# Unit length of queries and keys as columns in a gated DeltaNet mixer

## The chip, the cores and the metric

The kernel runs on one core of one Trainium2 chip. The metric is the device time of one execution in microseconds (us), shown as the median of several runs. A profiled execution is one further run of the same program, with its instructions recorded. "Span" is the time from its first to its last instruction; the execution's own time is a little longer.

## What is computed

A decoder trunk of two layers on 272 tokens (16 learned ones and 256 given) of width 1024. Each layer is a mixer and then a mixture of experts (MoE) whose weights fill most of the memory traffic. The change is in the second layer's mixer, a gated DeltaNet with 8 heads of queries and keys, 16 of values, width 128:

```python
q, k, v = jnp.split(jax.nn.silu(causal_depthwise_conv(qkv, conv_w)), ...)
q = jnp.repeat(l2_normalize(q.reshape(B, T, 8, 128)), 2, axis=2)   # x * rsqrt(sum(x*x) + 1e-6)
k = jnp.repeat(l2_normalize(k.reshape(B, T, 8, 128)), 2, axis=2)
g, beta = -exp(a_log) * softplus(a + dt_bias), sigmoid(b)
# per chunk of 64 tokens, gc = cumsum(g), decay[i,j] = exp(gc_i - gc_j):
m   = tril((k * beta) @ k.T * decay, -1)
sol = triangular_solve(m + eye, [v * beta, k * beta * exp(gc)])     # -> u, w
v_new = u - w @ S
o     = (q * 128**-0.5 * exp(g)) @ S + (q * 128**-0.5) @ k.T * decay @ v_new
S     = S * exp(g_last) + (k * exp(g_last - g)).T @ v_new
```

The output o then goes through an RMS norm per head, a gate and the output projection.

## The kernel before

All engines work from one program that is issued in a written order; each engine runs its own part of it in that order. The engines: PE (matrix products into PSUM), DVE (VectorE), ACT (ScalarE), POOL (GpSimd), SP (issues the transfers).

`mixer1` runs 48 projections of 128 columns, numbered m: keys' heads (m = 0 to 7), queries' heads (8 to 15), values (16 to 31), gates z (32 to 47). Each is 24 matmuls (`proj3`, line 361), since the operands are split into a high and a low part: ACT or DVE writes the high part of a weight tile (lines 72 and 74, `HI1`), mostly POOL the low part (line 347, `LO1`), two projections ahead (`ahead`). Weight tile 20 is written into the memory that the squares of the queries (tile `s`) held before. After projection m, `conv` copies the result to SBUF (ACT, line 838), takes the four taps of the short convolution (ACT line 840, DVE three times line 842), and the silu of the result before it (ACT, line 856) writes the head to `qk` and gives the PSUM bank free. There are 8 PSUM banks for everything.

Between the projections, pieces of other work are issued. They are Python generators, and the table `PLAN` says after which m each takes its next step: `clear`, `places`, `residual`, `uk` = `unit(8)` (the keys' length), `ga` = `heads` (gates, strengths beta in `bt`, decays), `dec` = `decay` (POOL line 1002, PE line 1007, ACT's Exp line 1008, DVE line 1013), and `uq` = `unit(0)` (the queries' length), in this order within one m. The products of keys with keys (`keys`) come at m = 14, 15 and 17, those with queries (`queries`) at 23 to 26 (both line 1029), the transposed keys (`key_rows`) at 15 to 19, the transposed values (`value_rows`, line 1217, scaled by beta in line 1221) at 21, 25 and 31 and after. From m = 15 the triangular systems are solved on DVE in the background (`systems`, `system0`, paced by `tick`), then joined on PE (`merges`, lines 1150 to 1186, with DVE's line 1166 between). After projection 33 the recurrence over five chunks follows (`read`, `solve`, `write`), in between the rest of the z projections and the first transfers of MoE weights into memory that has become free, then the output projection, then the MoE.

`unit(i0)` normalises eight heads in nine steps. In four steps ACT squares two heads each (line 882). In the fifth, PE sums each head's squares over the partitions into one row of a bank (line 888), ACT takes Ln and Exp(-0.5 x) of the 128 x 272 result (lines 892 and 893; each needs another activation table), and DVE splits the factor into a high and a low part (lines 74 and 347, tile `sq`). In the last four, for each head two matmuls with a column of `sel8` spread its factor over all partitions (line 899), and DVE multiplies the head by it (line 902).

`heads` picks the gates of the heads out as columns by small products with the identity (line 918) and ends with `nbe`, minus decay times beta (line 955). In the recurrence `nbe` scales what is read from the state (line 1306), `eg` the queries' part (line 1308), and line 1351 adds that to the part inside the chunk.

Of the kernel before, what the change touches and what calls it, by code (L numbers as in the profile page):

```python
# [8 lines left out]
F32 = mybir.dt.float32  # L9
# [4 lines left out]
OP = mybir.AluOpType  # L14
# [30 lines left out]
HX = 24  # L45
EXTRA = (3, 1, 1, 1, 1, 3)
NTS = 650
PLAN = ((0, 0, 1, 1, 3), (1, 4), (6, 10), (5, 6, 7, 8, 9, 11, 12, 13, 13), (0, 0, 2, 3, 7, 8), (6, 8, 9, 10, 11), (11, 13, 14, 16, 18, 20, 21, 22, 22))
HI1 = 'aaaaaaaavavvvaavaaaaaaaaaaaaaaavaavavaaaaavavaaa'
LO1 = 'ppppppppppppppppppppppppppppppppppvvppppppppppvp'  # L50
ZN = 21
# [2 lines left out]
class Trunk:  # L54
# [24 lines left out]
    def constants(self):  # L79
# [30 lines left out]
        nc.gpsimd.memset(self.col, 0.0)  # L110
        nc.gpsimd.memset(self.col[:, 1:2], 1.0)
        self.ones = self.col[:, 1:2].to_broadcast([128, 128])
        self.sel8 = c.tile([128, 8], F32, name="sel8")
        nc.vector.tensor_copy(self.sel8.bitcast(F32R).rearrange("p (a g) -> p g a", a=2),
                              self.ident.rearrange("p (g a) -> p g a", g=4)[:, :, 0:2])
        self.neghalf = c.tile([128, 2], F32, name="neghalf")
        nc.gpsimd.memset(self.neghalf, -0.5)
        self.lnst = c.tile([128, 3, 4, 6], F32, name="lnst")
# [622 lines left out]
    def mixer1(self):  # L741
# [10 lines left out]
        def tl(shape, name, bufs=1, pl=None):  # L752
            return (pl or qp).tile(shape, F32, tag=name, name=name, bufs=bufs)
# [12 lines left out]
        Abd, qk = cut(ab_, 0, (5, 8, 128)), cut(qk_, 0, (16, T))  # L766
        ktok = [cut(ab_, 5120, (4, 128)), cut(ab_, 5632, (4, 128))] + [cut(tk, 512 * i, (4, 128)) for i in range(3)]
        g, gs, nbe = cut(tk, 1536, (5, 8)), tk[:, 1576:1736], tk[:, 1736:1776]
        bvs = {}

        def bv(c, h, n=1):
# [99 lines left out]

        def unit(i0):

            ts = slice(0 if i0 else 16, T)
            if i0:
                s = [tl([128, 640], f"vt{i // 2}", 2, ep) for i in range(4)]
                s = [s[i // 2][:, T * (i % 2):T * (i % 2) + T] for i in range(8)]
            else:
                s = self.half(0, "s").rearrange("p (h t) -> p h t", h=8)
                s = [s[:, i, :] for i in range(8)]  # L880
            for i in range(8):
                nc.scalar.activation(s[i][:, ts], qk[:, i0 + i, ts], AF.Square)
                if i % 2:
                    yield
            p = self.ps()
            for i in range(8):
                a, r = i // 4, 32 * (i % 4)
                nc.tensor.matmul(p[r:r + 32, ts], self.col[:, 1 - a:33 - a], s[i][:, ts], start=(a == 0), stop=(a == 1),
                                 skip_group_check=True)
            f = tl([128, T], "cv", 1, ep)[:, ts]  # L890
            fh, fl = (tl([128, T], "sq", 2, ep)[:, ts] for _ in range(2))
            nc.scalar.activation(f, p[:, ts], AF.Ln, bias=eps6)
            nc.scalar.activation(f, f, AF.Exp, scale=-0.5)
            self.split(fh, fl, f, "v", "v")
            yield
            for i in range(8):
                p = self.ps()
                for a in (fh, fl):
                    nc.tensor.matmul(p[:, ts], self.sel8[:, i:i + 1].to_broadcast([128, 128]).bitcast(F32R),
                                     a.bitcast(F32R), start=(a is fh), stop=(a is fl))  # L900
                o = qk[:, i0 + i, ts]
                V.scalar_tensor_tensor(o, o, 1.0 if i0 else 128.0 ** -0.5, p[:, ts], op0=OP.mult, op1=OP.mult)
                if i % 2:
                    yield

        def heads():

# [44 lines left out]
            V.tensor_sub(gs[:, 40:80], pg[:, 40:80], gs[:, 0:40])  # L952
            yield
            nc.scalar.activation(gs, gs, AF.Exp)
            V.scalar_tensor_tensor(nbe, gs[:, 0:40], -1.0, bt.rearrange("p c h -> p (c h)"), op0=OP.mult, op1=OP.mult)
            yield

        eg, egl, eS = gs[:, 0:40], gs[:, 40:80], gs[:, 80:160]

        def residual():  # L960

# [100 lines left out]
        def system0():  # L1062
# [3 lines left out]
            nc.gpsimd.memset(M0, 0.0)  # L1066
            unit_matrix(X0, 16)
            yield 1200
            V.tensor_copy(b0[:, 0:8], bt[:, 0, :])
            bs0 = tl([128, 32], "bs", 1, pp)  # L1070
            V.transpose(out=bs0, in_=b0)
            for hf in range(2):
# [30 lines left out]

        def systems():

            V.transpose(out=bs, in_=bt[:, 1:5, :].rearrange("p c h -> p (c h)"))
            V.transpose(out=Ms, in_=KT[:, :, 0:32].rearrange("p s i -> p i s"))
            yield 2000

# [24 lines left out]
            for hf in range(2):  # L1134
                r0, r1 = slice(64 * hf, 64 * hf + 32), slice(64 * hf + 32, 64 * hf + 64)
                V.transpose(out=M21[r1], in_=KT[r0, :, 32:64])
                nc.gpsimd.tensor_tensor(M21[r1], M21[r1], bt[r1, 1:5, :].rearrange("p c h -> p (c h)")[:, :, None]
                                        .to_broadcast([32, 32, 32]), op=OP.mult)
                yield 1200

# [69 lines left out]
        def value_rows(b):  # L1210
            for c0 in (0, 2, 4):
# [6 lines left out]
                for c in range(c0, c0 + cn):  # L1218
                    for j in range(2):
                        o = 256 * (c - c0) + 128 * j  # L1220
                        nc.scalar.activation(bv(c, 2 * b + j)[:, 0, :], p[:, o:o + 128], AF.Copy,
                                             scale=bt[:, c, 2 * b + j:2 * b + j + 1])

        nz = [0]

# [103 lines left out]
        def write(c, b):  # L1329
# [18 lines left out]
                nc.tensor.matmul(pv[:, 256 + 128 * s:384 + 128 * s], Abd[:, c, 2 * b + s, :], vn[:, s, :],  # L1348
                                 start=True, stop=True)
            o = bv(c, 2 * b, 2)  # L1350
            V.tensor_tensor(o, pv3[:, 2:4], yd, op=OP.add)
            t3 = st[c, b] = tl([128, 3, 2], "ost", 3, rp)
            for s in range(2):
                junk = tl([128, 128], "junk", 2, rp)
# [871 lines left out]
```

## Time and profile before

| | us |
|---|---|
| median of 3 runs | 1351.94 |
| lowest and highest run | 1349.91, 1352.54 |
| profiled execution, own time | 1349.69 |
| its span | 1347.9 |
| busy in the span: PE, PEld | 1192.5, 694.3 |
| busy in the span: DVE, ACT, POOL | 452.6, 341.6, 204.7 |
| mean granted PE clock | 0.935 of 2.4 GHz |

PE is the matmuls, PEld the loads of their weights, which overlap them. A line number is one of the listing; a helper's line (72, 74, 347, 361) stands for all its callers. A matmul of full float32 operands is recorded as two instructions. In a timeline a row is a group of equal instructions: start, length, engine, line, operation, tiles, shape, count, and in brackets how long the engine had stood idle before and what ended that. Groups of matmuls overlap their neighbours, so the time that one takes is read from start to start.

### The profile page before, as it was taken

The numbers are of one execution on the slowest core, as the hardware profiler recorded it, in microseconds if no ns is written. First come the engines' busy times: TensorE is split into PE (matmuls) and PEld (weight loads), VectorE is DVE, ScalarE is ACT, GpSimd is POOL, SyncE is SP. The second block draws the span as 40 slices with busy tenths as digits, with TensorE's granted clock in tenths as the row PEclk, the third lists the DMA queues.
The fourth block names the chain that finished last, engine by engine and source line by source line (L and its number), as shares of the span: only waits on it lengthen the run. The fifth ranks groups of instructions, "written<-read, shape, count | busy, mean of one in ns | idle before, by whom it ended". The sixth has DMA issues, their size and how long they took to land. (4 is left out here: it accounts for less than half of the span.)

```text
span 1347.9 us, 19704 instructions
## 1 busy us (share of the span) xinstructions
PE 1192.5 (88%) x8074; PEld 694.3 (52%) x8074; DVE 452.6 (34%) x1035; ACT 341.6 (25%) x739; POOL 204.7 (15%) x183
## 2 busy tenths in 40 slices
PE   9999998898899799899999999899787868968786
PEld 9877544242435244378888878784231323414132
DVE  4876321010110201148987376653010010101013
ACT  4763110000100000057575645432010010101001
POOL 5621000000000000048754453000000000000000
PEclk9999998979697987999998999999999998998889
DMA  8599799999999999934333344979999999999996
GB/s 265 151 344 361 293 417 423 423 427 424 421 425 426 424 424 426 383 112 154 103 117 97 126 157 164 389 290 407 421 427 427 427 425 424 426 426 427 427 424 245
DMA packets 129844, 454.92 MB, mean 338 GB/s; under 512 B 19667, under 2 KB 62390, under 8 KB 94918
## 3 DMA queue, kind: packets, MB, share of 16 engines
q1 hardware_dynamic: 129590, 452.95, 84.4%
q8 instruction: 67, 1.10, 0.3%
q10 hardware_dynamic: 144, 0.52, 0.1%
q14 instruction: 43, 0.35, 0.1%
HBM read 452.39 MB, written 1.05 MB: 336 GB/s over the span
## 5 line engine op out<-in xcount | busy, mean ns | idle before, releaser
L1907 PE MATMUL ps<-Sg,h 128*128 128x128 f32 (+1 forms) x640 | 170.4, 409 | 11.8 <-ACTq L2179 11.5
L1907 PEld LDWEIGHTS ps<-Sg,h 128*128 128x128 f32 (+1 forms) x640 | 143.4, 291 | 56.9 <-issue 30.1
L1931 PE MATMUL ps<-w,xg 128*32 128x512 f32 x456 | 137.1, 636 | 10.3 <-DMA w<-in_moe_w_up_dram 10.0
L2037 DVE TENSOR_TENSOR acc<-acc,ps 128x512 f32<-128x512 f32 x48 | 33.0, 688 | 234.4 <-PE ps L2028 234.4
L347 POOL TENSOR_TENSOR w<-w 128x1024 fp32r<-128x1024 f32 x14 | 33.3, 2380 | 477.0 <-ACT w L72 467.7
L295 DVE TENSOR_SCALAR xg<-ps,pg 128x128 f32<-128x128 f32 x66 | 24.2, 406 | 219.2 <-PE ps L1907 218.0
L1952 DVE TENSOR_TENSOR y<-y,ps 128x512 f32<-128x512 f32 x16 | 11.0, 688 | 225.9 <-PE ps L1931 225.9
L253 POOL TENSOR_SCALAR lnmv<-lnmv 128x1 f32<-128x1 f32 (+2 forms) x9 | 2.6, 294 | 523.8 <-DVE lnmv L320 523.2
L1931 PE MATMUL ps<-wr,xg 128*32 128x512 f32 x320 | 80.2, 655 | 1.4 <-DMA wr<-in_moe_w_up_dram 1.4
L2028 PE MATMUL ps<-y,ct 128*128 128x512 f32 (+1 forms) x170 | 77.1, 584 | 2.1 <-ACT y L72 2.1
L1931 PE MATMUL ps<-we,xg 128*32 128x512 f32 x304 | 71.3, 620 | 7.1 <-DMA we<-in_moe_w_up_dram 7.1
L361 PE MATMUL ps<-xh,ws 128*128 128x272 f32 (+2 forms) x496 | 73.1, 293 | 2.7 <-ACT ws L72 2.6
L293 ACT ACTIVATE xg<-ps,pg 128x128 f32<-128x128 f32 x62 | 25.1, 453 | 190.0 <-PE ps L1907 190.0
L1931 PE MATMUL ps<-wb,xg 128*32 128x512 f32 x264 | 71.2, 677 | 0.5 <-DMA wb<-in_moe_w_up_dram 0.5
L347 POOL TENSOR_TENSOR ws<-w,ws 128x1024 fp32r<-128x1024 f32 x26 | 61.9, 2387 | 56.1 <-ACT ws L72 43.5
L361 PEld LDWEIGHTS ps<-xh,ws 128*128 128x128 f32 (+1 forms) x496 | 65.4, 189 | 4.5 <-ACT ws L72 2.8
L1931 PE MATMUL ps<-tb,xg 128*32 128x512 f32 x152 | 60.2, 627 | 5.6 <-DMA tb<-in_moe_w_up_dram 5.6
L1931 PEld LDWEIGHTS ps<-w,xg 128*32 128x32 f32 x456 | 31.2, 116 | 64.5 <-issue 45.5
L72 ACT ACTIVATE hT<-ps 128x512 f32<-128x512 f32 x16 | 9.6, 597 | 199.9 <-PE ps L1956 199.9
L1989 PE MATMUL ps<-w,hT 128*32 128x512 f32 x144 | 52.3, 652 | 8.7 <-DMA w<-in_moe_w_down_dram 8.0
L72 ACT ACTIVATE y<-ps 128x512 f32<-128x512 f32 (+1 forms) x34 | 19.4, 572 | 153.8 <-PE ps L1989 125.0
L842 DVE SCALAR_TENSOR_TENSOR ps<-xp,cw,ps 128x272 f32<-128x272 f32 (+1 forms) x96 | 47.6, 498 | 21.7 <-ACT ps L840 20.0
(518 smaller groups left out, 2266.5 us busy)
## 6 DMA issues: line engine op xcount, KB each, us to landing
w<-in_moe_w_up_dram SPq DMA_DIRECT2D x34, 1024.0 KB, 19.6
w<-in_odd_w_in_dram SPq DMA_DIRECT2D x24, 1024.0 KB, 5.2
w<-in_moe_w_gate_dram SPq DMA_DIRECT2D x23, 1024.0 KB, 19.6
wr<-in_moe_w_gate_dram SPq DMA_DIRECT2D x22, 1024.0 KB, 17.9
we<-in_moe_w_down_dram SPq DMA_DIRECT2D x22, 1024.0 KB, 17.9
we<-in_moe_w_gate_dram SPq DMA_DIRECT2D x20, 1024.0 KB, 10.6
wr<-in_moe_w_down_dram SPq DMA_DIRECT2D x20, 1024.0 KB, 19.6
wr<-in_moe_w_up_dram SPq DMA_DIRECT2D x18, 1024.0 KB, 21.1
```

The costliest lines, as they stand in the source:

```text
L72: self.nc.scalar.activation(out, in_, AF.Copy)
L293: self.nc.scalar.activation(out, in_, AF.Identity, scale=g, bias=b)
L295: self.nc.vector.tensor_scalar(out, in_, g, b, op0=OP.mult, op1=OP.add)
L347: e.tensor_tensor(lo.bitcast(F32R), x, hi, op=OP.subtract)
L361: self.nc.tensor.matmul(p[0:m, t0:T], w[:, k, 0:m], x[:, k, n0:], start=(n == order[0] and k == 0), stop=(n == order[2] and k == 7))
L842: V.scalar_tensor_tensor(cv, x[:, j + t0:j + T], w(j), cv, op0=OP.mult, op1=OP.add)
L1907: nc.tensor.matmul(p[:, 128 * j:128 * j + 128], self.rows(k.H(t), k0 + j, gr), Sg[0:P, t].rearrange("p e c -> p (e c)"), start=(t == 1), s ...
L1931: nc.tensor.matmul(pp[s, :], xg[:, kk + r, s], w[:, j, r, :], start=(kk + r == 0), stop=(kk + r == 7), skip_group_check=True)
L1952: V.tensor_tensor(hid, hid, pu, op=OP.mult)
L1989: nc.tensor.matmul(pys[h][s, :], hT[:, kf + r, s], w[:, j, r, 512 * h:512 * h + 512], start=(kf + r == 0), stop=(kf + r == 3), skip_group_ ...
L2028: nc.tensor.matmul(p, ct[:, t0:t0 + P], y, start=not (end and t), stop=True, skip_group_check=bool(end and t))
L2037: V.tensor_add(a, a, parts[t])
```

## The change

Queries and keys stay as the convolution gives them. `unit` copies the sums of squares to SBUF (tile `f`), and in the next step picks them out, token by partition and head by column, with small products whose weights are 64 columns of `f`; it takes Ln and Exp of 40 (keys) or 32 (queries) columns. For the keys this gives `bt2`, beta over the squared length, in place of beta in the systems and in `nbe`, and `bt1`, beta over the length, in place of beta for the values. For the queries it gives `fq`, one over the length times 128^-0.5, which goes into `eg` and into line 1351. `sel8` goes, and `PLAN` changes for `unit`, which now has seven steps, and for no other generator.

```diff
-PLAN = ((0, 0, 1, 1, 3), (1, 4), (6, 10), (5, 6, 7, 8, 9, 11, 12, 13, 13), (0, 0, 2, 3, 7, 8), (6, 8, 9, 10, 11), (11, 13, 14, 16, 18, 20, 21, 22, 22))
+PLAN = ((0, 0, 1, 1, 3), (1, 4), (6, 10), (5, 6, 7, 8, 9, 10, 11), (0, 0, 2, 3, 7, 8), (6, 8, 9, 10, 11), (11, 13, 14, 16, 17, 18, 19))
-        self.sel8 = c.tile([128, 8], F32, name="sel8")
-        nc.vector.tensor_copy(self.sel8..., self.ident...)
+        bt1, bt2, fq = (tk[:, o:o + 40] for o in (1776, 1816, 1856))
...
-            f = tl([128, T], "cv", 1, ep)[:, ts]
-            fh, fl = (tl([128, T], "sq", 2, ep)[:, ts] for _ in range(2))
-            nc.scalar.activation(f, p[:, ts], AF.Ln, bias=eps6)
-            nc.scalar.activation(f, f, AF.Exp, scale=-0.5)
-            self.split(fh, fl, f, "v", "v")
+            f = tl([128, T], "cv", 1, ep)
+            nc.scalar.activation(f[:, ts], p[:, ts], AF.Copy)
             yield
-            for i in range(8):
-                p = self.ps()
-                for a in (fh, fl):
-                    nc.tensor.matmul(p[:, ts], self.sel8[:, i:i + 1].to_broadcast([128, 128]).bitcast(F32R),
-                                     a.bitcast(F32R), start=(a is fh), stop=(a is fl))
-                o = qk[:, i0 + i, ts]
-                V.scalar_tensor_tensor(o, o, 1.0 if i0 else 128.0 ** -0.5, p[:, ts], op0=OP.mult, op1=OP.mult)
-                if i % 2:
-                    yield
+            p, c0 = self.ps(), 0 if i0 else 1
+            for c in range(c0, 5):
+                for hf in range(2):
+                    pick = self.ident.rearrange("p (z q j) -> p q j z", z=2, q=2)[:, hf, 0:2, :, None]
+                    nc.tensor.matmul(p[64 * hf:64 * hf + 64, 8 * c:8 * c + 8], f[:, CST[c]:CST[c] + 64],
+                                     pick.to_broadcast([128, 2, 2, 2]), start=True, stop=True, skip_group_check=True)
+            p = p[:, 8 * c0:40]
+            nc.scalar.activation(p, p, AF.Ln, bias=eps6)
+            if i0:
+                nc.scalar.activation(bt2, p, AF.Exp, scale=-1.0)
+                nc.scalar.activation(bt1, p, AF.Exp, scale=-0.5)
+                yield
+                b40 = bt.rearrange("p c h -> p (c h)")
+                V.tensor_tensor(bt2, bt2, b40, op=OP.mult)
+                V.tensor_tensor(bt1, bt1, b40, op=OP.mult)
+                V.scalar_tensor_tensor(nbe, eg, -1.0, bt2, op0=OP.mult, op1=OP.mult)
+            else:
+                nc.scalar.activation(fq[:, 8:40], p, AF.Exp, scale=-0.5)
+                yield
+                V.tensor_scalar(fq[:, 8:40], fq[:, 8:40], 128.0 ** -0.5, None, op0=OP.mult)
+                V.tensor_tensor(eg[:, 8:40], eg[:, 8:40], fq[:, 8:40], op=OP.mult)
+            yield
...
-            V.scalar_tensor_tensor(nbe, gs[:, 0:40], -1.0, bt.rearrange("p c h -> p (c h)"), op0=OP.mult, op1=OP.mult)
...
-            V.tensor_tensor(o, pv3[:, 2:4], yd, op=OP.add)
+            V.scalar_tensor_tensor(o, pv3[:, 2:4], fq[:, j:j + 1], yd, op0=OP.mult, op1=OP.add)
```

In `system0`, `systems` (and its M21) `bt` becomes `bt2`, and in line 1221 it becomes `bt1`; shapes stay.

## Rows read from the trace of the kernel before

**Rows 1.** The page's slices: the span in 40 equal parts, each digit the busy share in tenths; DMA is the mean busy share of the 16 DMA engines.

```profile
PE   9999998898899799899999999899787868968786
...
DMA  8599799999999999934333344979999999999996
```

**Rows 2.** Busy time by stage. Columns: the stretch and its length, then busy us of PE, PEld, DVE, ACT and POOL with the number of instructions, the granted clock of PE as a share of 2.4 GHz, the DMA share and GB/s.

```profile
640.00:705.00 65.00, 60.04 (x535) 56.10 (x534) 59.06 (x129) 42.92 (x95) 41.03 (x22) 0.97 0.37 114
705.00:765.00 60.00, 58.84 (x1147) 54.61 (x1146) 36.97 (x83) 37.24 (x92) 28.02 (x19) 0.94 0.36 109
765.00:838.00 73.00, 73.00 (x554) 57.43 (x554) 46.57 (x120) 35.05 (x115) 31.85 (x33) 1.00 0.41 144
...
905.00:1310.00 405.00, 328.46 (x1862) 129.40 (x1862) 48.98 (x108) 37.79 (x75) 0.00 (x0) 0.94 1.01 421
```

**Rows 3.** Waits of SP, which issues the transfers, from 838 to 1340 us: what waited for what, us in total, times, longest. Line 1691 issues MoE weights.

```profile
SPq L1691 <- PE ps L1931: 32.6, 20, 12.1
...
SPq L1691 <- DVE xp L347: 22.1, 4, 5.8
```

**Rows 4.** Timeline of PE in the stage of the change, and its first wait in the merges. Columns: start us, us, engine, line, operation, tiles, shape, count, idle before.

```profile
635.01 3.13 PE L1007 MATMUL ps<-R,lstrict 128*128 128x512 f32 x6 [1.05 <-POOL R L1002]
...
646.50 0.60 PE L899 MATMUL ps<-sq,sel 128*128 128x272 f32 x2 [1.23 <-DVE qk L902]
646.91 2.05 PE L361 MATMUL ps<-xh,tb 128*128 128x260 f32 x8
...
651.32 1.16 PE L899 MATMUL ps<-sq,sel 128*128 128x272 f32 x8
652.99 1.22 PE L361 MATMUL ps<-xh,bv 128*128 128x260 f32 x8 [0.50 <-ACT qk L856]
...
656.06 1.55 PE L1029 MATMUL ps<-qk 128*64 128x64 f32 x32
657.54 1.22 PE L361 MATMUL ps<-xh,bv 128*128 128x260 f32 x8
...
660.62 1.15 PE L1029 MATMUL ps<-qk 128*64 128x64 f32 x32
...
674.31 1.07 PE L888 MATMUL ps<-s,col 128*32 128x256 f32 x16
...
684.97 1.27 PE L361 MATMUL ps<-xh,bv 128*128 128x272 f32 x8 [1.19 <-ACT vt L856]
...
690.07 1.31 PE L1217 MATMUL ps<-ident,vt 128*128 128x128 f32 x10 [1.37 <-ACT vt L856]
...
694.24 1.09 PE L899 MATMUL ps<-sq,sel 128*128 128x256 f32 x8
...
699.42 1.32 PE L1029 MATMUL ps<-qk 128*64 128x64 f32 x8 [0.29 <-DVE qk L902]
...
730.33 1.20 PE L1183 MATMUL ps<-TX,Ms 32*32 32x32 f32 x64 [1.16 <-DVE TX L1166]
```

**Rows 5.** Busy time in short stretches around the wait of 1.23 us; columns as in rows 2.

```profile
645.00:647.00 2.00, 0.77 (x5) 0.50 (x4) 1.93 (x6) 1.97 (x5) 2.00 (x2) 0.95 0.00 0
647.00:649.00 2.00, 2.00 (x11) 2.00 (x11) 1.94 (x4) 0.42 (x2) 2.00 (x1) 0.50 0.41 54
```

**Rows 6.** Timeline of DVE: the two splits of the factor, the keys' and the queries'.

```profile
636.00 1.12 DVE L74 CAST sq<-cv 128x272 fp32r<-128x272 f32 x1 [3.12 <-ACT cv L893]
637.15 0.44 DVE L347 TENSOR_TENSOR sq<-cv,sq 128x272 fp32r<-128x272 f32 x1
...
681.11 0.29 DVE L74 CAST sq<-cv 128x256 fp32r<-128x256 f32 x1 [0.80 <-ACT cv L893]
681.44 0.42 DVE L347 TENSOR_TENSOR sq<-cv,sq 128x256 fp32r<-128x256 f32 x1
```

**Rows 7.** Groups of DVE's instructions by line and shape, 580 to 850 us. Columns: line, engine, operation, tiles, shapes, count, then busy us and mean ns of one, then the idle time before them and what ended it.

```profile
L1306 DVE SCALAR_TENSOR_TENSOR r<-ps,tk,bv 128x128 f32<-128x128 f32 x24 | 8.3, 348 | 14.1 <-PE ps L1301 8.8 <-ACT yd L1308 5.3
...
L1351 DVE TENSOR_TENSOR bv<-ps,yd 128x256 f32<-128x256 f32 x12 | 5.0, 417 | 0.0
...
L902 DVE SCALAR_TENSOR_TENSOR qk<-qk,ps 128x272 f32<-128x272 f32 x8 | 3.0, 431 | 0.0
L902 DVE SCALAR_TENSOR_TENSOR qk<-qk,ps 128x256 f32<-128x256 f32 x8 | 2.9, 411 | 0.0
...
L244 DVE TENSOR_TENSOR ps<-ps,sp 128x40 f32<-128x40 f32 x6 | 1.2, 206 | 0.2
```

**Rows 8.** Timeline of PE where `heads` picks the gates out (line 918), with the instructions behind it.

```profile
597.75 0.76 PE L918 MATMUL ps<-ident,sq 32*64 32x16 f32 x20 [0.48 <-ACT sq L913]
598.44 1.27 PE L361 MATMUL ps<-xh,tb 128*128 128x272 f32 x8
```

**Rows 9.** Timeline of ACT: a table load and the activation behind it, and the high part of weight tile 20.

```profile
632.44 1.28 ACT L892 ACT_TABLE_LOAD   x1
633.74 0.49 ACT L892 ACTIVATE cv<-ps,eps 128x272 f32<-128x272 f32 x1
...
675.50 1.06 ACT L72 ACTIVATE ws<-w 128x1024 fp32r<-128x1024 f32 x1 [1.70 <-issue]
```

More of the change, by code (lines that the diff above doesn't have):

```diff
@@ L112, in constants @@
         self.ones = self.col[:, 1:2].to_broadcast([128, 128])
-        self.sel8 = c.tile([128, 8], F32, name="sel8")
-        nc.vector.tensor_copy(self.sel8.bitcast(F32R).rearrange("p (a g) -> p g a", a=2),
-                              self.ident.rearrange("p (g a) -> p g a", g=4)[:, :, 0:2])
         self.neghalf = c.tile([128, 2], F32, name="neghalf")
@@ L768, in mixer1 @@
         g, gs, nbe = cut(tk, 1536, (5, 8)), tk[:, 1576:1736], tk[:, 1736:1776]
+        eg, egl, eS = gs[:, 0:40], gs[:, 40:80], gs[:, 80:160]
+        bt1, bt2, fq = (tk[:, o:o + 40] for o in (1776, 1816, 1856))
         bvs = {}
@@ L954, in heads @@
             nc.scalar.activation(gs, gs, AF.Exp)
-            V.scalar_tensor_tensor(nbe, gs[:, 0:40], -1.0, bt.rearrange("p c h -> p (c h)"), op0=OP.mult, op1=OP.mult)
             yield
-        eg, egl, eS = gs[:, 0:40], gs[:, 40:80], gs[:, 80:160]
         def residual():
@@ L1068, in system0 @@
             yield 1200
-            V.tensor_copy(b0[:, 0:8], bt[:, 0, :])
+            V.tensor_copy(b0[:, 0:8], bt2[:, 0:8])
             bs0 = tl([128, 32], "bs", 1, pp)
@@ L1104, in systems @@
         def systems():
-            V.transpose(out=bs, in_=bt[:, 1:5, :].rearrange("p c h -> p (c h)"))
+            V.transpose(out=bs, in_=bt2[:, 8:40])
             V.transpose(out=Ms, in_=KT[:, :, 0:32].rearrange("p s i -> p i s"))
@@ L1136, in systems @@
                 V.transpose(out=M21[r1], in_=KT[r0, :, 32:64])
-                nc.gpsimd.tensor_tensor(M21[r1], M21[r1], bt[r1, 1:5, :].rearrange("p c h -> p (c h)")[:, :, None]
+                nc.gpsimd.tensor_tensor(M21[r1], M21[r1], bt2[r1, 8:40, None]
                                         .to_broadcast([32, 32, 32]), op=OP.mult)
@@ L1221, in value_rows @@
                         nc.scalar.activation(bv(c, 2 * b + j)[:, 0, :], p[:, o:o + 128], AF.Copy,
-                                             scale=bt[:, c, 2 * b + j:2 * b + j + 1])
+                                             scale=bt1[:, 8 * c + 2 * b + j:8 * c + 2 * b + j + 1])
         nz = [0]
```

## The prediction, on record before the change was run

> **What bounds the kernel now.** I read the slices of the profile's page first, to see which resource is full in which part; then the busy time by stage; then the timelines of PE, VectorE (DVE) and ScalarE (ACT) in the stage that the change touches; last the waits of the DMA queue, to see whether time saved there reaches the end. In the slices the reader is to see two regimes: the transfers are full in most of the span and fall to about a third in the second mixer, where PE is full instead [rows 1]. By stage, PE is busy 60.04 of the 65 us from 640 to 705, and DVE 59.06: both are near their limit, and each makes the other wait. From 705 to 838 PE is busy 131.84 of 133 us, and DVE far less; from 905 to 1310 the DMA share is 1.01 [rows 2]. So time taken off the stretch 640 to 705 is kept if PE stays the bound up to 838 and the transfers of the expert weights start earlier by as much. They do: between 838 and 1340 the DMA queue waits, besides for itself, for PE and DVE to give slots free (32.6 and 22.1 us in the largest such rows) [rows 3]. The transfers follow the compute out of the mixer; I let a microsecond saved there count as one at the end.
>
> **What goes, PE.** `unit` spreads each head's factor over the partitions by two matmuls, 32 in all (line 899). Eight keys' take 1.16 us, eight queries' 1.09 [rows 4], so 2 x 1.16 + 2 x 1.09 = 4.50 us. They also bring waits, as each pair needs a PSUM bank and DVE has to empty it: 1.23 us before the second pair of a step, and 0.29 before queries' products that need a scaled head [rows 4]. After the 1.23 us the granted clock falls from 0.95 to 0.50, that is from nearly always 2.4 to 1.2 GHz [rows 5]: the projection behind it takes 646.91 to 651.32 = 4.41 us, where one at full clock takes 657.54 to 660.62 = 3.08, a loss of 1.33 [rows 4]. Three more waits, 0.50, 1.19 and 1.37 = 3.06 us, end with the silu of a convolution (line 856), which waits for DVE or for ACT's tables [rows 4].
>
> **What goes, DVE.** Sixteen scalings (line 902): 3.0 + 2.9 = 5.9 us [rows 7]. The two splits of the factor: 1.12 + 0.44 + 0.29 + 0.42 = 2.27 us, and in front of them DVE stands still 3.12 and 0.80 us for ACT's Exp, with the convolutions of the next heads queued behind [rows 6]. Together 12.1 us of DVE's 65.
>
> **What comes, PE.** Eighteen little products pick the squares' sums out as columns. The nearest row is the same pick for the heads' gates (line 918): ten calls, 20 instructions, start 597.75, next start 598.44, so 34.5 ns each [rows 8]. Eighteen calls are 36 instructions: 1.24 us. Below it lies 0.55 us: the keys' twenty run ahead of the second decay products, where PE waits 1.05 us for POOL anyway [rows 4], so they may cost nothing, and sixteen are left. Above it lie the products of line 1029, 64 weight columns and 64 moving ones, 32 in 1.55 us: 36 x 48 = 1.74 us [rows 4]. I take 1.24, the same shape. A rule speaks for more: the Trainium skill (TensorE: Matmul & The Clock Gate, LDWEIGHTS) gives columns / 1.2 ns for a weight load, 53 ns for 64 columns, by which the picks would come to 1.9 us as an estimate. The row of the existing pick does not bear that out.
>
> **What comes, DVE.** Five small operations on 32 or 40 columns at 0.21 us [rows 7]; one of them, the negated strengths, is only moved, so four are new: 0.8 us. The copy of `sel8` at the start goes, off the path. The sum of line 1351 becomes a scalar_tensor_tensor. Before it is 417 ns; the nearest rows of the new kind are 411 ns with a constant (line 902) and, with a column but half the elements, 348 (line 1306) [rows 7]. Scaled by elements beyond the half, a column costs 420 to 460 ns. Sixteen times 0 to 0.04 us lie beside PE, which is busy all of 765 to 838 [rows 2]; only the last group's stands before the output projection: 0 to 0.1 us, I take 0.1. The strengths that the systems, the values and M21 read are of the same shape as before: nothing.
>
> **What moves.** Per unit, ACT copies 272 or 256 columns where it took Ln, and takes Ln and Exp of 40 or 32 columns one step later. The keys' Ln and Exp now stand directly before the decay's Exp, so one change to silu and back falls away, two table loads. A load is 1.28 us and the activation starts 0.02 after it [rows 9]: 2.6 us of ACT. The Trainium skill (ScalarE: Activation LUTs, What ACT_TABLE_LOAD costs) adds a drain of 1.38 us to each; no gap of that length follows the load here, and by it the queries' three loads would hold ACT longer, which speaks for rival A. The sums of the queries are taken at projection 17, not 18. They read the tile whose memory the split of weight tile 20 overwrites; ACT now waits 1.70 us for them (675.50) [rows 9], just behind the sums (674.31) [rows 4], and that wait goes. No DMA is issued by a moved step; POOL's splits stay where they are. New waits: PE's picks wait for ACT's copy of the step before; Ln waits for the picks. At the keys the copy is ready a projection early. At the queries it stands behind a silu that waits for DVE, and the next projections of PE are queued behind the picks; this may cost up to the 0.5 us that such a wait took at 652.99 [rows 4].
>
> **Sum.** PE's own work: -4.50 + 1.24 = -3.26. The waits tied to the scaled heads and the clock: -1.23 - 0.29 - 1.33 = -2.85. Of the 3.06 us on silu I take back 2.4: DVE has 12.1 - 0.8 us less in its way, but the queries' three table loads still stand in ACT's queue, and half of the 1.19 us that follows them stays. The line 1351 tail adds 0.1. Together -3.26 - 2.85 - 2.4 + 0.1 = -8.4 us. The profiled execution took 1349.69 us (span 1347.9 and 1.8 around), so it would take 1341.3; the median of the runs, 1351.94, stands 2.25 higher, and I forecast the median: 1343.5 us. Bounds: all three waits go and the keys' picks are free, -3.26 - 0.69 - 2.85 - 3.06 = -9.9; only the work goes, at the dear pick, -4.50 + 1.74 = -2.8. What is late next is PE itself in the projections.
>
> **Rivals.** *A, only PE's work goes.* The waits belong to ACT's table loads and POOL's order, and come again at other places; 0.69 to 1.74 us of picks against 4.50, and the first wait half gone: about -4, so 1348. For it: three loads stay at the queries, and POOL's 1.05 us stays [rows 4]. Against it: the largest wait and the half clock name line 902, which is gone. Chance 0.20.
> *B, the gain is given back.* PE arrives earlier at the merges and waits longer for DVE's line 1166, where it already waits 1.16 us [rows 4], or the weights' transfers do not start earlier: 0 to -2, so 1351. Against it: DVE is relieved by more than PE, and is busy only 36.97 of 60 us there [rows 2]. Chance 0.12.
> *C, slower.* The queries' picks wait for ACT's copy at projection 18, the granted clock falls as it does after the 1.23 us, and the half clock lasts through the value projections, whose small key products keep PE loosely filled. At 1.33 us per projection the gain of 8.4 is eaten after six or seven; from nine on (12.0) the kernel is slower by over 0.2%: about 1355.5. Against it: after 1.19 and 1.37 us of waiting in the same stretch no projection was slowed. Chance 0.06.
>
> **How the numbers follow.** My forecast (-6 to -12, the waits gone in most part) has 0.62, and its number is 1343.5. The low end: the bound -9.9, the 1.16 us at the merges, which a freer DVE may shorten, and 1.3 us for the spread of the median's runs (1349.91 to 1352.54), so 1339.5. The high end: rival A and the same spread, 1349.5. Outside lie most of B, all of C and a rest below. The measurement of this kernel can tell about 0.2% (2.7 us) from no change: the forecast and most of A lie beyond it, B and the end of A within. Faster 0.80, same 0.14, slower 0.06.
>
> **What would show it.** Right: PE's starts from the second decay products (635.01) to the queries' products at 699.42 [rows 4] stand 8 to 9 us closer; no half clock behind a scaled head; about 1.2 us of picks in two groups; DVE busy some 52 us where it was 59.06; everything behind earlier by the same amount, the last weights' transfers too. Wrong: PE's waits on silu as long as before (A); a longer wait for line 1166, or the main run of expert weights no earlier than before (B); granted clock 0.5 behind the queries' picks (C).

## The result: slower by 0.7%, and the profile after

| | before | after |
|---|---|---|
| median, us | 1350.39 (5 runs) | 1359.78 (5 runs) |
| lowest to highest | 1346.45 to 1352.54 | 1359.17 to 1363.22 |
| span of the profiled execution | 1347.9 | 1358.0 |

The ratio is 1.0073, with a 95% interval from 1.0057 to 1.0089. The forecast, 1343.5, lies on the wrong side, and its range ends 10 us too low.

To find where the time went I cut each span into three sections: up to the first projection of the second mixer; from there to the start of the last product of the recurrence (line 1357 of the kernel after); and the rest, which is mostly layer 1's experts. All starts are read from PE's timelines; GB/s is read from the windows 150 to 550 us (layer 0's experts) and 905 to 1300 us (layer 1's). The experiments are in the same table, since all of them are read in this way. Each set of experiments has runs of the kernel before of its own (medians 1348.95 to 1350.24 us), and each ratio is to those; two executions, one of before (1548.12 us) and one of e3 (3411.31 us), were far slower than all others and are in no ratio. "Moved by" says where the left-hand weight tiles lie in SBUF, in bytes per partition against before.

| kernel | moved by | to 1st projection | mixer | rest | GB/s, layers 0 and 1 | ratio to before, 95% |
|---|---|---|---|---|---|---|
| before | 0 | 591.0 | 251.7 | 505.2 | 422, 421 | 1 |
| after | -32 | 597.2 | 246.0 | 514.8 | 418, 416 | 1.0073 [1.0057, 1.0089] |
| e1 | 0 | 591.3 | 242.6 | 504.5 | 422, 425 | 0.9979 [0.9969, 0.9989] |
| e8 (e1 again) | 0 | 592.4 | 246.6 | 506.0 | 422, 423 | 0.9966 [0.9949, 0.9983] |
| e2 | +32 | 599.6 | 249.9 | 513.9 | 417, 416 | 1.0109 [1.0089, 1.0130] |
| e3 | -64 | 596.4 | 246.3 | 513.6 | 418, 415 | 1.0067 [1.0051, 1.0082] |
| e4 | 0 | 593.3 | 240.8 | 505.3 | 422, 425 | 0.9925 [0.9912, 0.9938] |
| e5 | -256 | 594.7 | 240.6 | 505.6 | 422, 425 | 0.9935 [0.9913, 0.9958] |
| e6 | -128 | 601.6 | 241.5 | 512.7 | 418, 417 | 1.0037 [1.0022, 1.0052] |
| e7 | -32 | 595.6 | 242.8 | 514.7 | 418, 416 | 1.0057 [1.0036, 1.0078] |
| e9 | -256, others too | 593.9 | 239.7 | 505.9 | 424, 425 | 0.9911 [0.9891, 0.9931] |
| e10 | 0 | 591.4 | 241.2 | 507.4 | 422, 425 | 0.9946 [0.9927, 0.9964] |
| e11 | 0, constants -32 | 591.3 | 242.7 | 506.3 | 422, 425 | 0.9941 [0.9922, 0.9960] |
| e12 | 0 | 592.4 | 257.7 | 505.6 | 422, 423 | 1.0070 [1.0047, 1.0094] |

After against before: +6.2, -5.7 and +9.6 us, together the +10.1 by which the spans differ. The mixer, the only place where arithmetic changed, did become shorter. The loss lies in the two sections that the forecast did not look at. Sections are of one profiled execution each; the first and the mixer of one and the same kernel differ by 1 and 4 us between e1 and e8, and e1's profiled execution (1340.2 us) was the fastest of its 14. Taken over all profiles the outer sections still fall into two groups: with the left-hand weight tiles where they were or 256 bytes away (nine profiles) the last section takes 504.5 to 507.4 us and the first 591.0 to 594.7; with them 32, 64 or 128 bytes off (five profiles) 512.7 to 514.8 and 595.6 to 601.6.

The page's slices show what those sections have in common. GB/s of each fortieth of the span before, then after with the DMA share above it, which answers to [rows 1]:

```profile
GB/s 265 151 344 361 293 417 423 423 427 424 421 425 426 424 424 426 383 112 154 103 117 97 126 157 164 389 290 407 421 427 427 427 425 424 426 426 427 427 424 245
```

```profile
DMA  8689799999999999935433436989999999999996
GB/s 251 163 336 354 309 409 418 420 420 421 418 420 420 421 420 420 382 118 155 125 94 97 155 125 234 352 314 409 413 420 419 420 417 418 419 420 420 420 414 223
```

In every slice in which the transfers are full, from the 7th to the 16th and from the 29th to the 39th, the rate is 3 to 10 GB/s lower. The transfers are as full as before (digits 9) and move less per us. The first of these stretches ends some 90 us ahead of the first instruction that the change touches, the copy of `sel8` at the start apart.

The mixer after, PE's timeline, with the rows that answer to [rows 4] and [rows 8] (projections are line 358 here, the picks 899, the silu 856, POOL's split 344; in the experiments up to 5 more):

```profile
639.99 0.76 PE L899 MATMUL ps<-ident,cv 128*64 128x8 f32 x20
640.84 2.13 PE L1016 MATMUL ps<-R,lstrict 128*128 128x512 f32 x4
643.28 1.13 PE L1016 MATMUL ps<-R,lstrict 128*128 128x512 f32 x2 [0.32 <-POOL R L1011]
...
689.80 1.16 PE L358 MATMUL ps<-xh,w 128*128 128x272 f32 x8
693.85 1.50 PE L358 MATMUL ps<-xh,ws 128*128 128x272 f32 x8 [2.89 <-ACT vt L856]
695.14 2.01 PE L358 MATMUL ps<-xl,ws 128*128 128x272 f32 x8
696.96 1.69 PE L358 MATMUL ps<-xh,ws 128*128 128x272 f32 x8
698.58 0.69 PE L1038 MATMUL ps<-qk 128*64 128x64 f32 x16
```

The twenty keys' picks take 639.99 to 640.84 = 0.85 us. The waits of 1.23 and 0.29 on scaled heads and the half clock behind the first are gone, as are the three silu waits of 0.50, 1.19 and 1.37. In their place stands one of 2.89, and behind it a projection that takes 693.85 to 698.58 = 4.73 us instead of 3.08, 1.65 lost to the lower clock (0.58 granted from 696.0 to 698.5 us). The same moment on all engines tells why:

```profile
685.98 2.39 POOL L344 TENSOR_TENSOR w<-w 128x1024 fp32r<-128x1024 f32 x1 [1.32 <-ACT w L72]
...
686.17 2.36 DVE L914 TENSOR_SCALAR tk<-tk 128x32 f32<-128x32 f32 x1
...
688.45 2.39 POOL L344 TENSOR_TENSOR ws<-w,ws 128x1024 fp32r<-128x1024 f32 x1
688.56 2.33 DVE L915 TENSOR_TENSOR tk<-tk 128x32 f32<-128x32 f32 x1
...
690.81 0.49 DVE L842 SCALAR_TENSOR_TENSOR ps<-xp,cw,ps 128x272 f32<-128x272 f32 x1
...
693.34 0.46 ACT L856 ACTIVATE vt<-ps 128x16 f32<-128x16 f32 x2 [4.84 <-DVE ps L842]
```

Two of DVE's four new operations, on 32 columns, take 2.36 and 2.33 us. Each begins while POOL splits a weight tile and ends as POOL's instruction ends (685.98 + 2.39 = 688.37 and 688.53; 688.45 + 2.39 = 690.84 and 690.89). The convolution's taps (line 842) are queued behind them, the silu waits 4.84 us for the taps, and PE for the silu. The other two new operations, the keys' on 40 columns, also have both operands in SBUF, but begin when POOL's instruction has ended (646.96 + 2.40 = 649.36, the next starts at 651.53) and take 0.20 us each:

```profile
646.96 2.40 POOL L344 TENSOR_TENSOR tb<-w,tb 128x1024 fp32r<-128x1024 f32 x1 [1.40 <-ACT tb L72]
...
649.67 0.20 DVE L908 TENSOR_TENSOR tk<-tk,bt 128x40 f32<-128x40 f32 x1
```

The waits of PE at the merges, 590 to 780 us of after (engine, tile, line, what it waited for, us in total, times, longest):

```profile
PE ps L1171 <- issue: 3.5, 2, 2.7
PE ps L358 <- ACT vt L856: 2.9, 1, 2.9
...
PE ps L1159 <- issue: 0.7, 1, 0.7
```

The 1.16 us for DVE [rows 4] are gone, but 4.2 us of standing still that no semaphore explains ("issue") have come. They come and go from profile to profile of one kernel: none in e1, 2.7 us in e8.

### The profile page after: what moved, and what is told of

The parts are those of the page before. It is cut to its first block, busy times and chain, and to the rows that moved or that the text cites. A ratio compares the mean times of both kernels' runs of the same rounds, so it can differ in the third digit from the quotient of the medians.

```text
span 1358.0 us, 19700 instructions
## 1 busy us (share of the span) xinstructions
PE 1184.2 (87%) x8078; PEld 688.8 (51%) x8078; DVE 450.3 (33%) x1018; ACT 338.1 (25%) x740; POOL 204.4 (15%) x183
## 4 chain that ended last, share of the span: by engine, by line
DMA 40%; PE 24%; DVE 5%; ACT 2%; SPq 1%; issue 1%; POOL 1%; DVEq 0%; ACTq 0%; POOLq 0%
PE ps L358 6%; DMA we<-in_moe_w_up_dram 4%; DMA w<-in_moe_w_down_dram 4%; PE ps L1536 3%; DMA we<-in_moe_w_down_dram 3%; DMA bv<-in_moe_w_up_dram 3%; DMA wb<-in_moe_w_gate_dram 3%; PE ps L1916 3%; PE ps L1940 3%; DMA ab<-in_moe_w_up_dram 2%; DMA tb<-in_moe_w_gate_dram 1%; DMA tb<-in_moe_w_up_dram 1%; DMA ab<-in_moe_w_gate_dram 1%; DMA bv<-in_moe_w_gate_dram 1%; DMA S<-in_moe_w_down_dram 1%; DMA w<-in_moe_w_gate_dram 1%
## 5 line engine op out<-in xcount | busy, mean ns | idle before, releaser
L1940 PE MATMUL ps<-w,xg 128*32 128x512 f32 x456 | 139.1, 643 | 13.0 <-DMA w<-in_moe_w_up_dram 10.9
L1940 PE MATMUL ps<-we,xg 128*32 128x512 f32 x304 | 74.8, 648 | 8.7 <-DMA we<-in_moe_w_up_dram 8.7
## 6 DMA issues: line engine op xcount, KB each, us to landing
we<-in_moe_w_gate_dram SPq DMA_DIRECT2D x20, 1024.0 KB, 10.5
```

The lines of the kernel that those rows point to most:

```text
L1940: nc.tensor.matmul(pp[s, :], xg[:, kk + r, s], w[:, j, r, :], start=(kk + r == 0), stop=(kk + r == 7), skip_group_check=True)
```

## The experiments

Two theories were open. By the first, the rate of the transfers fell because the 32 bytes of `sel8` are gone: in the memory plan of the compiled program every left-hand tile behind `sel8` lies 32 bytes lower. The weight tiles `w` stood at 55296, 63488 and 71680, all multiples of 256, and stand at 55264 and so on. By the second, something that the change computes slows what follows. A third question was what the two long operations of DVE cost.

**e1, the 32 bytes put back.** The kernel after, with nothing else changed than these lines (the tile is written and never read):

```diff
+        self.sel8 = c.tile([128, 8], F32, name="sel8")
+        nc.vector.tensor_copy(self.sel8.bitcast(F32R)..., self.ident...)
```

> The changed kernel with the 32-byte constant tile sel8 and its copy put back, unused, so that every tile behind it lies where it lay before the change. Theory P (place): the change took 32 bytes out of the constants, so every weight tile behind them starts 32 bytes past a multiple of 64, and the expert weights' transfers run about 1.2% slower (419 to 420 GB/s for 423 to 425 in layer 0); the mixer itself is 5.7 us shorter. Expected: ratio to the kernel before 0.9958 (about 1344.7 us for 1350.4), first projection of the mixer at 591 us, 421 GB/s or more from 905 to 1310 us. Rival S (steps): the new steps in the mixer and what they trigger cost the time, the place is nothing: ratio 1.007, first projection at 597 us.

1347.1 us (14 runs; 1344.7 was expected). The outer sections are back at 591.3 and 504.5 us, the rates at 422 and 425. The long operations of DVE (2.36 and 2.34) and PE's wait of 2.89 are still there.

**e2, the kernel before, moved up.** No instruction differs:

```diff
-        self.sel8 = c.tile([128, 8], F32, name="sel8")
+        self.sel8 = c.tile([128, 16], F32, name="sel8")[:, 0:8]
```

> The kernel before with sel8 32 bytes longer (its first 8 columns used), so that all tiles behind it start 32 bytes past a multiple of 64, no instruction changed. Theory P: as slow in the transfers as the changed kernel, about 1350.4 + 15.8 = 1366 us (ratio 1.012), first projection near 597 us. Rival S: ratio 1.000.

1365.18 us (6 runs): 32 unused bytes make the kernel before slower by 1.1%. Its windows, and those of before and after (stretch, length, busy us of PE, PEld, DVE, ACT, POOL, granted clock, DMA share, GB/s), in the order before, after, e2:

```profile
150.00:550.00 400.00, 357.27 (x1924) 155.51 (x1920) 64.47 (x127) 35.09 (x71) 0.00 (x0) 0.88 1.01 422
905.00:1300.00 395.00, 321.07 (x1830) 127.85 (x1830) 48.98 (x108) 37.79 (x75) 0.00 (x0) 0.94 1.01 421
```

```profile
150.00:550.00 400.00, 353.57 (x1890) 154.04 (x1892) 64.51 (x127) 34.76 (x70) 0.00 (x0) 0.89 1.01 418
905.00:1300.00 395.00, 313.65 (x1803) 127.81 (x1802) 49.32 (x109) 37.20 (x74) 0.00 (x0) 0.96 1.01 416
```

```profile
150.00:550.00 400.00, 354.11 (x1886) 153.20 (x1886) 64.21 (x126) 34.80 (x70) 0.00 (x0) 0.88 1.02 417
905.00:1300.00 395.00, 313.42 (x1818) 129.56 (x1821) 52.68 (x131) 40.22 (x77) 1.53 (x6) 0.96 1.01 416
```

**e3, 64 bytes instead of 32.** The kernel after, with the tiles `validh` and `neghalf` laid in one:

```diff
-        self.validh = c.tile([128, 1], F32, name="validh")
+        vn = c.tile([128, 8], F32, name="validh")
+        self.validh, self.neghalf = vn[:, 0:1], vn[:, 2:4]
...
-        self.neghalf = c.tile([128, 2], F32, name="neghalf")
```

> The changed kernel with another 32 bytes taken out (two small constants share one slot), so that tiles lie 64 bytes before their old place: multiples of 64 again, but no longer the multiples of 512 that several were. Theory P with a grain of 64 bytes: ratio 0.996, about 1344.7 us. Theory P with a coarser grain (128 to 512 bytes): like the changed kernel or between, 1350 to 1360. Rival S: 1.007.

1358.15 us (median of the five runs in the ratio), as slow as after: a multiple of 64 does not help.

**e6 and e5, 128 and 256 bytes.** On e4's kernel (below), a constant is moved to the other end of SBUF, which also pushes the right-hand tiles down by its size: `iota1` (128 bytes) in e6, `onesb` (256 bytes) in e5.

```diff
+        self.constr = ctx.enter_context(tc.tile_pool(name="constr", bufs=1, side="right"))
...
-        self.iota1 = c.tile([128, 32], F32, name="iota1")
+        self.iota1 = self.constr.tile([128, 32], F32, name="iota1")
```

> As e5 with a constant of 128 bytes: tiles start 128 bytes before their place. Theory P with a grain of 128 bytes (64 was too little, e3): as e4, 0.9925. With a grain of 256 or 512: slow, about 1.003, and 416 GB/s in layer 1's experts in place of 425.

> As e4, with a constant of 256 bytes moved to the other end of the memory, so that every weight tile of layer 1 and every unmoved constant's successor starts 256 bytes before its place in the kernel before; no instruction changed. Theory P with a grain of 256 bytes or less: as e4, ratio 0.9925. Theory P with a grain of 512: transfers slow again, ratio 0.9925 + 0.011 = 1.003 or so. A rival to P altogether (each layout has its own chance time): anything, with no order among the shifts.

e6: 1354.55 us, rates 418 and 417. e5: 1340.22 us, 422 and 425. Moves by 32, 64 and 128 bytes cost, one by 256 does not. The Trainium skill (DMA: Bandwidth & Descriptors, How a descriptor splits into AXI transactions) says of reading that a transaction must start at a multiple of 256 bytes, and that a descriptor which starts elsewhere begins at the boundary below and spends beats on bytes it does not use. The grain of 256 agrees; that it holds for the place written in SBUF, and what it costs over whole tiles, is what these runs add.

**e11, only the weight tiles put back.** e7's kernel with a gap of 32 bytes behind the activations, so constants and activations stay 32 bytes lower:

```diff
+        ctx.enter_context(tc.tile_pool(name="gap", bufs=1)).tile([128, 8], F32, name="gap")
         self.wa = ctx.enter_context(tc.tile_pool(name="wa", bufs=1))
```

> The kernel of e7 (sel8 gone, both factors read from PSUM; 1356.39 us) with 32 unused bytes right ahead of the weight tiles: the constants behind sel8 and the nine activation buffers of the main pool stay 32 bytes lower, as in the change, and the weight tiles and what lies behind them stand where they stood before the change. Theory: the places of the tiles that weights are loaded into set the rate of their transfers; then 422 GB/s from 150 to 550 us and 425 from 905 to 1300, the last section (recurrence's end to the span's end) 504 to 507 us, the time 1338 to 1343 us. Rival: what the compute engines read and write at the new addresses (constants, activations) slows the kernel; then 418 and 416 GB/s, 512 to 515 us and 1353 to 1358.

1342.35 us:

```profile
150.00:550.00 400.00, 357.59 (x1924) 156.01 (x1920) 64.02 (x124) 35.20 (x71) 0.00 (x0) 0.88 1.01 422
905.00:1300.00 395.00, 316.05 (x1798) 123.84 (x1790) 47.39 (x104) 35.25 (x71) 0.00 (x0) 0.95 1.01 425
```

So neither the addresses of the constants nor those of the activations matter here, but those of the tiles that weights are loaded into, and what lies behind them. (By the plan some 3% of the expert weights land in the memory of the activations, and stay 32 bytes lower here.)

**e9, the rest aligned too.** Not all expert weights landed at multiples of 256 in before. By the memory plan eleven tiles of layer 0, the right-hand ones and the back buffers, stood at 192 modulo 256 and took 110 of the layer's 384 MB; all of layer 1's stood at multiples of 256 (the expectation counted eight and three). In e9 `sel8` is gone as in after, four small constants move to the right-hand end, and 64 unused bytes go ahead of the back buffers:

```diff
-        self.rev = c.tile([128, 32], F32, name="rev")
+        self.rev = self.constr.tile([128, 32], F32, name="rev")
...
+            self.cx.enter_context(self.k.tc.tile_pool(name="gap", bufs=1)).tile([128, 16], F32, name="gap")
         self.room(f"wb{self.l}", n)
```

> The kernel of e4 (both new factors' product read from PSUM) with every weight tile of the two layers at a multiple of 256 bytes: sel8 gone as in the change, the constants rev, thr8, validh and neghalf at the right end (together 256 bytes less on the left, 192 more on the right), and layer 0's back buffers 64 bytes up; before and in e4 layer 0's right-hand and back buffers and layer 1's right-hand ones stood at 192 modulo 256. No arithmetic is changed. If the start of a tile modulo 256 sets how fast its transfers go, 8 more tiles of layer 0 and 3 more of layer 1 go at the better rate: over 422 GB/s in 150 to 550 us (424 to 427), the mixer's first projection 2 to 5 us earlier than in e4 and the time 1334 to 1338 us. Rival: only the lower-left tiles count, or the rate depends on something else that e2, e3 and e6 moved at once: 422 GB/s and 1339 to 1341 as in e4 and e5.

1339.41 us, where 1334 to 1338 was expected. The rate of layer 0 rose as the theory wants, to 424, but the first projection came no earlier than in e4, and the time cannot be told from e4's: the intervals of the two ratios overlap. A half per cent of rate is where the time stops telling.

The rate itself tells more in windows that full transfers fill from end to end. Before, after, e9:

```profile
250.00:450.00 200.00, 173.31 (x908) 73.79 (x900) 23.56 (x42) 16.57 (x33) 0.00 (x0) 0.88 1.01 424
960.00:1290.00 330.00, 258.78 (x1340) 101.01 (x1344) 33.04 (x64) 28.09 (x57) 0.00 (x0) 0.93 1.01 426
```

```profile
250.00:450.00 200.00, 171.30 (x903) 72.78 (x899) 23.57 (x42) 16.68 (x33) 0.00 (x0) 0.88 1.01 420
960.00:1290.00 330.00, 251.44 (x1322) 98.29 (x1314) 32.47 (x62) 26.53 (x54) 0.00 (x0) 0.95 1.01 419
```

```profile
250.00:450.00 200.00, 174.13 (x936) 74.39 (x928) 23.55 (x42) 16.78 (x33) 0.00 (x0) 0.88 1.01 426
960.00:1290.00 330.00, 260.32 (x1362) 103.10 (x1362) 32.47 (x63) 27.74 (x56) 0.00 (x0) 0.93 1.01 426
```

From 960 to 1290 us the rate is 426 GB/s in all nine profiles of the first group and 419 or 420 in the five others; the 421 and 423 of the table come from a window that begins before the transfers are full. The trace shows the same packet by packet. A packet of 8 KB is one partition's row of a weight tile. In this window such packets take 309.6 ns on average in each of the nine profiles, and 314.1 to 315.3 ns in the five. From 250 to 450 us (layer 0) they take 309.7 ns in e9, 311.1 to 311.7 in the other eight and 314.3 to 315.0 in the five. So the transfer of a row itself takes longer, and layer 0 in before had paid a part of this price already.

**e4, DVE reads PSUM.** e1 with ACT's Exp left in its PSUM bank, so that both of DVE's operations read the factor there:

```diff
-                nc.scalar.activation(fq[:, 8:40], p, AF.Exp, scale=-0.5)
+                nc.scalar.activation(p, p, AF.Exp, scale=-0.5)
...
-                V.tensor_scalar(fq[:, 8:40], fq[:, 8:40], 128.0 ** -0.5, None, op0=OP.mult)
-                V.tensor_tensor(eg[:, 8:40], eg[:, 8:40], fq[:, 8:40], op=OP.mult)
+                V.tensor_scalar(fq[:, 8:40], p, 128.0 ** -0.5, None, op0=OP.mult)
+                V.scalar_tensor_tensor(eg[:, 8:40], p, 128.0 ** -0.5, eg[:, 8:40], op0=OP.mult, op1=OP.mult)
```

> As e1, and the queries' factor stays in PSUM: Exp writes the bank, and the two small DVE operations read it from there (the second as scalar_tensor_tensor). Theory W (wait for POOL): the two operations took 2.36 and 2.33 us for 0.2 because they took turns with POOL's split of a weight tile, and caused PE's wait of 2.89 us and the half clock behind it; with one operand in PSUM they take 0.2 to 0.3 us each, and the kernel is 3 to 4.5 us faster than e1 (about 1341). Rival: they are slow for another reason, or PE's wait has another cause: same time as e1 within 1 us.

1339.49 us (1338.67 to 1341.2), 7.6 less than e1 where 3 to 4.5 were expected. All engines at the same moment:

```profile
682.20 2.39 POOL L347 TENSOR_TENSOR w<-w 128x1024 fp32r<-128x1024 f32 x1 [1.32 <-ACT w L72]
682.38 0.18 DVE L917 TENSOR_SCALAR tk<-ps 128x32 f32<-128x32 f32 x1
682.47 0.18 DVE L918 SCALAR_TENSOR_TENSOR tk<-ps,tk 128x32 f32<-128x32 f32 x1
...
685.33 0.46 ACT L859 ACTIVATE vt<-ps 128x16 f32<-128x16 f32 x2 [0.62 <-DVE ps L845]
```

POOL runs as before, DVE's operations take 0.18 us, the silu waits 0.62 instead of 4.84, and PE's wait of 2.89 is gone. The Trainium skill (SBUF — State Buffer, SBUF: two separate sides) tells of a pair of ports that VectorE and GpSimd share, held by one of them for a whole instruction while the other is blocked; VectorE needs it with two inputs in SBUF or in a faster mode. The ends of the rows in after agree with that, and so does e4. The profiles show only a part of the 7.6 us: e1's is that of its fastest run, and its mixer is 1.8 us longer than e4's. In the six profiles with the factor read from PSUM (e4 to e7, e9, e11) the mixer takes 239.7 to 242.8 us, in the four with it in SBUF (after, e1, e3, e8) 242.6 to 246.6.

**e7, that alone.** The kernel after with e4's edit and no 32 bytes.

> The changed kernel, tiles at its own places (32 bytes early), with e4's two operations read from PSUM. If place and wait are two separate causes: e4 plus the cost of the place, 1339.5 + 12 to 16 = 1351 to 1356 (ratio 1.002 to 1.005). If the wait were the whole loss: 0.9925 as e4.

1356.39 us, against 1359.78: the mixer 242.8 instead of 246.0, the transfers as slow as after. The intervals of these two ratios overlap; what the wait costs is shown by e1 and e4, whose intervals do not. The two causes are separate: e7 has the slow transfers without the wait, e1 the wait without the slow transfers.

**e8, e1 once more**, beside e5 to e7.

> The kernel of e1 once more, since its profiled execution took 1340.2 and most of its other runs 1346 to 1348. If it has two times, a second profile may fall on the longer one and shows where the 7 us lie: the two waiting operations and the half clock behind them (theory W), or the transfers. Ratio 0.998 again.

1345.84 us. In the two sets e1's kernel is faster than before by 0.1 to 0.5% (both intervals). The mixer of this profile is 4.0 us longer than e1's, 2.7 of them the merges' standing still.

**e10 and e12, more picks.** e4 with each of the 36 picks issued four and eight times into the same place:

```diff
+                    for _ in range(8):
                         nc.tensor.matmul(p[64 * hf:64 * hf + 64, 8 * c:8 * c + 8], f[:, CST[c]:CST[c] + 64], ...
```

> The kernel of e4 with each of the 36 matmuls that turn the sums of squares into columns issued four times into the same place: 108 matmuls more, the output unchanged. The forecast counted TensorE work of this stage one for one (4.50 us of scaled heads out, 1.24 us of picks in at 34.5 ns each). If that counts on the path, 108 x 35 to 40 ns = 3.8 to 4.3 us are added to e4's 1339.5: 1343 to 1344. Rival: the picks' stretch lies beside a wait of VectorE or ScalarE that ends later anyway, then under 1.5 us is added: 1339.5 to 1341.

> The kernel of e4 with each of the 36 picks issued eight times, 252 matmuls more in two runs (140 and 112): 252 x 37.6 ns (e10: 80 in 3.01 us) = 9.5 us more TensorE work in the stage whose work the forecast counted one for one. e10's profile showed 4.0 us more work and 2.0 us less waiting in the mixer, its median 3.8 us more than e4. One for one: 1339.5 + 9.5 = 1349.0, and with the 2.2 us wait of the merges swallowed 1346.8: 1346 to 1350. Rival: VectorE or ScalarE set the mixer's end and TensorE's work there is worth half or less: 1339.5 to 1344.

e10: 1343.25 us, 3.8 more than e4 as expected, but the intervals of the two ratios overlap, and in the one profile the mixer grew by only 0.4, where 4.0 us of picks came in and e4's wait at the merges shrank from 2.2 to 0.5. e12: 1359.49, 20 us more where 6.5 to 10.5 were expected. PE's timeline, then windows of the same kernel:

```profile
635.28 9.48 PE L903 MATMUL ps<-ident,cv 128*64 128x8 f32 x160
...
681.22 8.12 PE L903 MATMUL ps<-ident,cv 128*64 128x8 f32 x128
689.27 0.48 PE L1071 MATMUL ps<-ident,qk 128*128 128x128 f32 x1
...
690.89 2.16 PE L361 MATMUL ps<-xh,w 128*128 128x272 f32 x8
```

```profile
635.00:640.00 5.00, 5.00 (x105) 4.86 (x105) 4.73 (x7) 2.42 (x4) 5.00 (x5) 1.00 0.67 218
640.00:645.00 5.00, 5.00 (x63) 4.98 (x62) 1.92 (x1) 0.20 (x1) 0.84 (x1) 0.55 0.00 0
...
685.00:690.00 5.00, 5.00 (x56) 4.90 (x56) 2.03 (x7) 0.58 (x1) 0.03 (x1) 0.50 0.01 3
```

160 and 128 picks hold PE for 9.4 and 8.1 us, not the 6.0 and 4.8 that 37.6 ns each would make: the granted clock falls to half inside each run, from 2.4 to 1.2 GHz, while PE does nothing else than 8-column products, and it is 0.50 behind them too (645 to 650 and 690 to 695 us). The picks alone are 16.1 us more than e4's 1.4, and the mixer grew by 16.9. So work of this size on PE in this stage reaches the end about one for one, and my sum of e12's price failed on the clock. For the 4 us of e10 only the medians say so, its profile does not.

## Why the prediction was wrong

**The step that failed** is one sentence: "The copy of `sel8` at the start goes, off the path." The copy is off the path; the tile is not. I counted the removal of a constant as nothing, and it moved every left-hand tile into which 1 MB weight transfers land. e2 prices that alone at 1.1%, 15 us; by sections of after it is 6.2 + 9.6 = 15.8 us. "No DMA is issued by a moved step" is true and did not ask where the transfers write. No range over the mixer's terms could hold this: it lies in the stages that the forecast took as fixed.

**The second step** is a term of the sum: "four are new: 0.8 us". They took 0.20, 0.20, 2.36 and 2.33 = 5.1 us, and brought the wait of 2.89 and 1.65 us of lower clock on PE. The durations were taken from rows whose operands lie in PSUM [rows 7], for operations on SBUF; the size held for the two that ran beside an idle POOL, and the other two took eleven times as much. A row read for another purpose showed the difference: the split of the factor took 1.12 us for the keys and 0.29 for the queries [rows 6], the same operation at nearly the same size. POOL's timeline of before has, beside the first of them:

```profile
633.92 3.04 POOL L1002 TENSOR_TENSOR R<-tk,mincl 128x512 f32<-128x512 f32 x3
```

It ends at 636.96, the split at 637.12. I used the 1.12 as a size without asking why it was not 0.29.

**What held.** PE's work: 32 spreading matmuls gone for 36 picks of 0.85 + 0.57 = 1.42 us, where I took 1.24 from a row of not quite the same shape (32 partitions and 16 columns [rows 8], where the new picks have 128 and 8); the dearer estimate of 1.9 was not borne out. The waits on scaled heads and their half clock went, and the three silu waits too. With both faults mended (e4) the mixer is 10.9 us shorter than before, where 8.4 were forecast and 9.9 was the bound, and the kernel takes 1339.49 us, 0.75% less than before. One profile's mixer can be 4 us off, so this bears out the direction and the rough size of the sum, not its terms one by one. Of the signs named, PE's starts from the second decay products to the queries' products (635.01 to 698.68 us before) stand 5.9 us closer in after (640.84 to 698.58) and 10.6 in e4 (637.05 to 690.10). DVE's busy time over the mixer falls from 180.7 us to 178.2 in after and 174.2 in e4; the "some 52 us" for 640 to 705 also took off the keys' split, which lies ahead of 640 [rows 6]. In the kernel after the mixer gave 5.7: DVE's two long operations and the merges' unexplained stops lie in it. Line 1360's sums cost 477 ns each instead of 417 [rows 7], 60 more where I had 0 to 40, and PE stays busy 72.98 of 73 us beside them.

**The rivals.** A: the silu waits did come at another place, once. It named ACT's table loads and POOL's order; it was held by two DVE operations that lasted as long as POOL's instruction. B's second sign came, expert weights no earlier than before (the recurrence's last product starts at 843.2 us, before at 842.7), but by slower transfers ahead of the mixer; its own cause did not, as PE does not wait for DVE at the merges in after. In e4 it does, for 2.2 us where before had 1.16, so with the faults mended a part of B is there. C, the only slower one, did not happen: the granted clock is 1.00 from 676 to 690 us, behind the queries' sixteen picks. A lower clock came behind the wait of 2.89 instead, for one projection where C needed nine. e10 shows 0.58 behind eighty picks and e12 0.50 to 0.55, but there the clock fell with PE busy, and C spoke of a wait. That the slower result came was thus not foreseen by the case that had the 0.06.

**Open:** what PE's "issue" stops at the merges are: 4.2 us in after, 2.7 in e8, 3.7 in e11, none in e1 and e4. No run was aimed at them. In the trace of after, transfers of the queues that carry instructions fall into the two at line 1171: one packet into the stop from 720.63 to 721.47 us (720.97 to 721.37), two into the one from 725.25 to 727.94 (725.35 to 726.48 and 727.00 to 727.31). That points at the loading of instructions, but such packets come without a stop too, so the cause is not shown. Also open is why e4 gains 7.6 us over e1. Not tried: which weight tiles weigh most, beyond e9.

## What to carry to other kernels

A removed or added tile is an edit to the address of everything allocated behind it: where transfers are full, compare the memory plans of both kernels, and keep the tiles that large transfers land in at multiples of 256 bytes, by a pad if need be. Look at the stretches that the change does not touch first: when the rate or length of one that ends ahead of the change differs, the cause is not in the changed instructions. Price a small DVE operation by a row with its operands in the same memory and with POOL as busy as it will be, and where two rows of nearly equal work differ almost fourfold, find out why before using either.

## What the runs showed of the hardware that I had not expected

- The rate of full transfers depends on where in SBUF they land: 422 to 424 GB/s (layer 0) and 421 to 425 (layer 1) with the left-hand weight tiles at multiples of 256 bytes, 417 to 418 and 415 to 417 with them 32, 64 or 128 bytes off (nine profiles against five). A packet of 8 KB takes 309.6 ns in the first case and 314.1 to 315.3 in the second (960 to 1290 us).
- A DVE operation on 128x32 with its inputs in SBUF, begun while POOL's instruction of 2.39 us runs, ends only with that one (2.36 and 2.33 us); with the factor in PSUM it takes 0.18 us beside the same instruction.
- Inside a run of 160 or 128 products of 8 columns the granted clock fell to half while PE was never idle: busy 5.00 of 5 us, granted 0.55 and 0.50.
